# Log-sum-exp of 16384 rows: the order, cutting and summing of the last sixteen rows of each partition

## The chip, the cores and the metric

The kernel runs on one core of a Trainium2 chip. The metric is the device time of one execution in microseconds; for a kernel it is the median over its runs. A core has TensorE (matrix products, accumulating in PSUM), VectorE, ScalarE (activation functions), GpSimd and SyncE, each with its own instruction stream, and sixteen DMA engines that move data between HBM and the on-chip memory SBUF. Streams meet only at semaphores. SBUF has 128 partitions; "columns" below are fp32 elements of one partition, so that one column over all partitions is 512 bytes.

## The reference

```python
x = np.random.randn(32, 512, 1024).astype(np.float32)

def reference(x):
    max_x = np.max(x, axis=-1, keepdims=True)
    return (max_x.squeeze(-1) + np.log(np.sum(np.exp(x - max_x), axis=-1))).astype(np.float32)
```

The input is 67.1 MB, read once. The output has 16384 numbers.

## The kernel before

**Data and rows.** The 16384 rows of 1024 columns are spread over 128 partitions, 128 rows for each. The first 112 rows of a partition (`W`) are contiguous in HBM, and so are the last 16 (`B`), in a second region. The kernel exponentiates without subtracting a maximum, sums, and takes the logarithm. A check of all sums goes with it: TensorE adds a number to the PSUM cell `count` for each sum that is out of bounds, and adds the sums themselves, so that anything not finite shows; VectorE compares `count` with a bound, and only if it fails the whole work is done again, with the maximum, in a branch at the end. With the data here the branch isn't taken.

**The ring.** The rows land in `ring`, 48 rows of each partition. SyncE issues every load on one queue, in program order. Before a load it waits (`load`, L133 to 147) until whoever last used that stretch of the ring is done, as noted in `users`. Eighteen loads are listed in `LOADS`, with their size in rows and what is done with them; the first is cut in two. The first nine have 16, 16, 16, 16, 13.5, 12.5, 9, 7 and 6 rows, which makes 112. They lie at ring rows 0, 16, 32; 0, 16, 29.5; 0, 9, 16. The last 16 rows lie at ring rows 22 to 38, in nine loads of 4576, 3328, 2528, 1856, 1344, 992, 736, 544 and 480 columns.

**Sums.** ScalarE exponentiates in place (L235), one activation for a group or a load. Then, by letter:

- R: VectorE sums whole rows (L246).
- F: GpSimd adds the two halves of each row (L240), and VectorE sums the halves later (`reduce_folded`, L177).
- T: VectorE folds a row on itself in one instruction and gets its sum from the accumulator (L256). All but the last of the late 16 rows go this way.
- Y and Z: the last row is cut in 544 and 480 columns. ScalarE exponentiates each into PSUM and takes the sum from its own accumulator (L209), into `first_sum` and `last_sum`. VectorE copies the first to SBUF (L219).

A load may end within a row; the row is then summed after the load that completes it.

**The end.** After row 119 is queued ScalarE takes the log of the 112 early sums (L275), and VectorE checks 119 sums (L152, L157). SyncE stores the 112 results once the load ahead of the last has landed (L285). ScalarE then takes the log of 15 late sums (L288), and of the last row as Ln(last_sum + first_sum), the first part as the bias operand (L290). The store of the 16 (L294) waits for it. In parallel VectorE checks nine sums (L299), and takes the maximum of the last piece's input over a ceiling (L310), which stands for the check of `last_sum`; TensorE adds these (L305 to L315), VectorE compares (L317), ScalarE and VectorE read the flag and report to SyncE (`done`). SyncE clears the semaphores and waits last for the store (L378).

The order of each engine's work is written out by hand in one loop over the loads; `Counted.wait` leaves out a wait that the same engine has already made.

Of the kernel before, what the change touches and what calls it, by code (L numbers as in the profile page):

```python
# [12 lines left out]
LOW, HIGH = 1e-15, 1e15  # L13
CEILING = 27.0
STEEP = 2.0**48
RING = 48
B = 16
LATE = 119
# [3 lines left out]

LOADS = [
# [3 lines left out]
]  # L29
# [25 lines left out]
def kernel(  # L55
# [5 lines left out]
    nc = tc.nc  # L61
# [17 lines left out]
    LAST = NC - 1  # L79
# [14 lines left out]
    assert sum(size for size, _ in loads) == NC * d  # L94
    assert sum(s for _, ops in loads for _, s in ops) == NC
# [5 lines left out]
    sumexp = sbuf("sumexp", NC)  # L101
    res = sbuf("res", NC)
    clamped = sbuf("clamped", NC)
    bad = sbuf("bad", 3)
    over = sbuf("over", d)
    far = sbuf("far", 1)
    ones = sbuf("ones", 1)
    steep = sbuf("steep", 1)
    less = sbuf("less", 1)
    fine = sbuf("fine", 1, i32, 1)  # L110
    last_exp = nc.alloc_psum_tensor("last_exp", [P, d], fp32).ap()
    first_sum = nc.alloc_psum_tensor("first_sum", [P, 1], fp32).ap()
    last_sum = nc.alloc_psum_tensor("last_sum", [P, 1], fp32).ap()
    count = nc.alloc_psum_tensor("count", [1, 1], fp32).ap()

    landed = [nc.alloc_semaphore(f"landed{i}") for i in range(len(loads))]
# [13 lines left out]
    dve.did(nc.vector.memset(steep, STEEP))  # L130
    less_at = dve.did(nc.vector.memset(less, -CEILING * (loads[-1][0] // 2)))

# [16 lines left out]
    def check_early():  # L149
        dve.wait(act, summed_by_act)  # L150
        dve.wait(dve, dve.n)
        dve.did(nc.vector.tensor_scalar(  # L152
            out=clamped[:, 0:LATE], in0=sumexp[:, 0:LATE],
            scalar1=LOW, scalar2=HIGH, op0=ALU.max, op1=ALU.min,
        ))
        dve.wait(dve, dve.n)
        dve.did(nc.vector.scalar_tensor_tensor(  # L157
            out=clamped[:, 0:LATE], in0=clamped[:, 0:LATE], scalar=0.0, in1=sumexp[:, 0:LATE],
            op0=ALU.bypass, op1=ALU.not_equal, accum_out=bad[:, 0:1],
        ))  # L160
# [3 lines left out]
    def add_up(c, who, **kw):  # L164
        pe.wait(*who)
        return pe.did(nc.tensor.matmul(count, lhsT=ones, rhs=sumexp[:, c : c + 1], **kw))  # L166
# [16 lines left out]

    c = 0
# [4 lines left out]
    summed_by_act = 0  # L189
    ln_early = None  # L190
    first_loads = []
    for i, (size, ops) in enumerate(loads):
        if here + size > RING * d:
            assert here == p
            p = here = 0
        if any(q < here + size and q + t * d > here for _, t, q, _ in folded):
            reduce_folded()
        dma = load(i, here, done_before, size)
        if i < AHEAD:
            first_loads.extend(x.ins for x in dma)  # L200
        end = here + size
        done_before += size
        act.wait(landed[i], 16 * len(dma))
        for k, (how, s) in enumerate(ops):
            rows = ring[:, p : p + s * d].rearrange("p (c d) -> p c d", d=d)
            if how in "YZ":

                assert c == LAST and (how == "Z" or here == p)
                at = act.did(nc.scalar.activation(  # L209
                    out=last_exp[:, here - p : end - p], in_=ring[:, here:end], func=AF.Exp,  # L210
                    accum_out=first_sum if how == "Y" else last_sum,
                ))
                if how == "Z":
                    last_piece = ring[:, here:end]
                here = end
                if how == "Y":
                    nc.vector.addr_align(128, offset=0, max_nops=0)
                    dve.wait(act, at)
                    first_piece = dve.did(nc.vector.tensor_copy(out=sumexp[:, LAST:NC], in_=first_sum))  # L219
                summed_by_act = at  # L220
            elif how == "A":
                assert here == p
                v = ring[:, p : p + d]
                at = act.did(nc.scalar.activation(
                    out=v, in_=v, func=AF.Exp, accum_out=sumexp[:, c : c + 1]
                ))
                here += d
                users.append((p, p + d, act, at))
                summed_by_act = at
                who = (act, at)  # L230
            else:

                upto = end if k + 1 == len(ops) and c + s < LAST else p + s * d
                v = ring[:, here:upto]
                at = act.did(nc.scalar.activation(out=v, in_=v, func=AF.Exp))  # L235
                here = upto
            if how == "F":
                reduce_folded()
                pool.wait(act, at)
                at = pool.did(nc.gpsimd.tensor_tensor(  # L240
                    out=rows[:, :, 0:H], in0=rows[:, :, 0:H], in1=rows[:, :, H:d], op=ALU.add
                ))
                folded.append((c, s, p, at))
            elif how == "R":
                dve.wait(act, at)
                who = (dve, dve.did(nc.vector.reduce_sum(  # L246
                    out=sumexp[:, c : c + s], in_=rows, axis=AX.X
                )))
                users.append((p, p + s * d, *who))
            elif how == "T":  # L250
                if c >= W:
                    reduce_folded()
                dve.wait(act, at)
                for r in range(s):
                    lo = rows[:, r, 0:H]
                    who = (dve, dve.did(nc.vector.scalar_tensor_tensor(  # L256
                        out=lo, in0=lo, scalar=1.0, in1=rows[:, r, H:d],
                        op0=ALU.mult, op1=ALU.add, accum_out=sumexp[:, c + r : c + r + 1],
                    )))
                    users.append((p + r * d, p + (r + 1) * d, *who))  # L260
                    if c + r >= LATE:
                        add_up(c + r, who, start=False, stop=False)
            if how == "A" and c >= LATE:
                add_up(c, who, start=False, stop=False)
            if how in "RT":
                if c < W:
                    early_sum = dve.n
                reduce_folded()
            c += s
            p += s * d  # L270
            if c == LATE:

                act.wait(dve, early_sum)
                act.wait(act, early_act)
                ln_early = act.did(nc.scalar.activation(  # L275
                    out=res[:, 0:W], in_=sumexp[:, 0:W], func=AF.Ln
                ))
                check_early()
            if c <= W:
                early_act = summed_by_act  # L280
        assert here == end
# [6 lines left out]
    act.did(nc.scalar.activation(out=res[:, W:LAST], in_=sumexp[:, W:LAST], func=AF.Ln))  # L288
    act.wait(act, summed_by_act)
    ln_last = act.did(nc.scalar.activation(  # L290
        out=res[:, LAST:NC], in_=last_sum, func=AF.Ln, bias=sumexp[:, LAST:NC]
    ))
# [4 lines left out]

    dve.wait(dve, dve.n)
    dve.did(nc.vector.scalar_tensor_tensor(  # L299
        out=clamped[:, LATE:NC], in0=sumexp[:, LATE:NC], scalar=LOW,  # L300
        in1=sumexp[:, LATE:NC], op0=ALU.max, op1=ALU.not_equal, accum_out=bad[:, 1:2],
    ))
    add_up(LAST, (dve, first_piece), start=False, stop=False)
    pe.wait(dve, dve.n)
    pe.did(nc.tensor.matmul(count, lhsT=bad[:, 1:2], rhs=far, start=False, stop=False))  # L305
    pe.wait(dve, less_at)
    pe.did(nc.tensor.matmul(count, lhsT=less, rhs=steep, start=False, stop=False))
    half = last_piece.shape[1] // 2
    dve.wait(landed[-1], 16)
    dve.did(nc.vector.scalar_tensor_tensor(  # L310
        out=over[:, 0:half], in0=last_piece[:, 0:half], scalar=CEILING,
        in1=last_piece[:, half : 2 * half], op0=ALU.max, op1=ALU.max, accum_out=bad[:, 2:3],
    ))
    pe.wait(dve, dve.n)
    at = pe.did(nc.tensor.matmul(count, lhsT=bad[:, 2:3], rhs=steep, start=False, stop=True))  # L315
# [117 lines left out]
```

## Time and profile before

| | us |
|---|---|
| median of 3 runs | 161.59 |
| lowest, highest | 161.46, 161.63 |
| the profiled execution, its own time | 161.57 |
| its span in the profile | 160.2 |
| VectorE busy | 114.3 |
| ScalarE busy | 114.5 |
| GpSimd busy | 37.3 |
| TensorE busy | 2.2 |
| ScalarE idle, waiting for loads | 42.3 |

The span runs from the first to the last record of the core; the 1.4 us between span and time lie before and behind it. A row of a timeline gives the start, the duration, the engine, the line of the kernel, the operation, what is written and read, and the shapes. A row of the chain of waits gives start, duration and what the program's end waited for then. Rows marked SPq are DMA issues by SyncE; "KB, us" behind an issue of the page are its size and the time from issue to landing. Windows give, for each stretch, busy time of TensorE, its weight loads, VectorE, ScalarE and GpSimd, then the clock share, the DMA share and GB/s.

### The profile page before, as it was taken

The page shows a single profiled execution, that of the slowest core. Times are in us where ns is not written, and L with a number is a line of the kernel's source. Part 1 is how long each engine was busy: PE and PEld are TensorE (multiplying, and loading weights), DVE is VectorE, ACT ScalarE, POOL GpSimd, SP SyncE. Part 2 cuts the span into 40 slices and gives each one's busy share as a digit, 9 for nine tenths or more (in the row PEclk, how much of TensorE's full clock was granted, in tenths as well). Part 3 has the DMA queues.
Part 4 walks back from the last instruction along what each step waited for, and adds up shares of the span by engine and source line. Part 5 has one row for each costly group of instructions (what it writes and reads, how often), then busy time and mean ns, then how long its engine had stood idle before and what let it go on. Part 6 is the DMA issues. An engine that isn't in the chain of part 4 may idle for free.

```text
span 160.2 us, 221 instructions
## 1 busy us (share of the span) xinstructions
PE 2.2 (1%) x26; PEld 1.1 (1%) x26; DVE 114.3 (71%) x59; ACT 114.5 (71%) x31; POOL 37.3 (23%) x11
## 2 busy tenths in 40 slices
PE   0000000000000000000000000000000000000022
PEld 0000000000000000000000000000000000000011
DVE  0000000009999499994999859959999999999996
ACT  3000059980799708995099949992999989799996
POOL 0000000000000000000000994690004969891000
DMA  9996996996996996997999999999999999999992
GB/s 319 507 460 301 507 524 262 524 524 262 524 524 262 524 524 262 524 474 311 483 442 442 442 425 409 409 409 471 423 414 417 458 409 399 444 412 428 415 408 97
DMA packets 3025, 67.18 MB, mean 419 GB/s; under 512 B 592, under 2 KB 720, under 8 KB 1488
## 3 DMA queue, kind: packets, MB, share of 16 engines
q1 hardware_dynamic: 3024, 67.18, 97.8%
q14 instruction: 1, 0.01, 0.0%
HBM read 67.11 MB, written 0.07 MB: 419 GB/s over the span
## 4 chain that ended last, share of the span: by engine, by line
DMA 51%; ACT 28%; DVE 19%; issue 1%; PE 0%
DMA ring<-in_x_dram 51%; ACT ring L235 28%; DVE sumexp L246 16%; DVE sumexp L177 2%; DVE ring L256 1%; DVE over L310 0%; PE count L315 0%; ACT res L275 0%; DVE clamped L299 0%; DVE fine L317 0%; DVE sumexp L219 0%
## 5 line engine op out<-in xcount | busy, mean ns | idle before, releaser
L235 ACT ACTIVATE ring<-ring 128x16384 f32<-128x16384 f32 (+16 forms) x23 | 111.7, 4908 | 42.3 <-DMA ring<-in_x_dram 42.3
L246 DVE TENSOR_REDUCE sumexp<-ring 128x16 f32<-128x16384 f32 (+4 forms) x9 | 85.6, 9513 | 42.1 <-ACT ring L235 42.1
L240 POOL TENSOR_TENSOR ring<-ring 128x3072 f32<-128x3072 f32 (+3 forms) x7 | 37.1, 5315 | 107.2 <-ACT ring L235 107.2
L177 DVE TENSOR_REDUCE sumexp<-ring 128x6 f32<-128x3072 f32 (+3 forms) x7 | 18.4, 2659 | 0.0
L256 DVE SCALAR_TENSOR_TENSOR ring<-ring 128x512 f32<-128x512 f32 x15 | 9.6, 687 | 0.4 <-ACT ring L235 0.4
L127 ACT ACT_TABLE_LOAD x1 | 1.3, 1283 | 1.9 <-PEq L64 1.9
L162 PE MATMUL count<-far,bad 128*1 128x1 f32 x2 | 0.2, 164 | 153.0 <-DVE clamped L157 153.0
L166 PE MATMUL count<-sumexp,ones 128*1 128x1 f32 x18 | 1.6, 164 | 3.6 <-DVE ring L256 3.6
L128 DVE MEMSET ones<- 128x1 f32 x1 | 0.1, 59 | 2.0 <-PEq L64 2.0
L256 DVE DVE_READ_ACCUMULATOR ring<-ring 128x1 f32 x15 | 1.2, 82 | 0.0
L209 ACT ACTIVATE last_exp<-ring 128x544 f32<-128x544 f32 (+1 forms) x2 | 1.2, 588 | 0.0
L162 PEld LDWEIGHTS count<-far,bad 128*1 128x1 f32 x2 | 0.1, 82 | 153.0 <-DVE clamped L157 153.0
L166 PEld LDWEIGHTS count<-sumexp,ones 128*1 128x1 f32 x18 | 0.8, 81 | 4.4 <-DVE ring L256 4.4
L310 DVE SCALAR_TENSOR_TENSOR over<-ring 128x240 f32<-128x240 f32 x1 | 0.4, 404 | 0.0
L317 DVE TENSOR_SCALAR fine<-count 1x1 int32<-1x1 f32 x1 | 0.1, 147 | 0.3 <-PE count L315 0.3
L157 DVE SCALAR_TENSOR_TENSOR clamped<-clamped,sumexp 128x119 f32<-128x119 f32 x1 | 0.3, 283 | 0.0
L275 ACT ACTIVATE res<-sumexp 128x112 f32<-128x112 f32 x1 | 0.3, 279 | 0.0
L290 ACT ACTIVATE res<-last_sum,sumexp 128x1 f32<-128x1 f32 x1 | 0.3, 261 | 0.0
L209 ACT ACTIVATION_READ_ACCUMULATOR last_exp<-ring 128x1 f32 x2 | 0.3, 129 | 0.0
L152 DVE TENSOR_SCALAR clamped<-sumexp 128x119 f32<-128x119 f32 x1 | 0.2, 222 | 0.0
L288 ACT ACTIVATE res<-sumexp 128x15 f32<-128x15 f32 x1 | 0.2, 213 | 0.0
L299 DVE SCALAR_TENSOR_TENSOR clamped<-sumexp 128x9 f32<-128x9 f32 x1 | 0.2, 170 | 0.0
(17 smaller groups left out, 1.8 us busy)
## 6 DMA issues: line engine op xcount, KB each, us to landing
ring<-in_x_dram SPq DMA_DIRECT2D x1, 7936.0 KB, 21.3
ring<-in_x_dram SPq DMA_DIRECT2D x1, 6912.0 KB, 23.9
ring<-in_x_dram SPq DMA_DIRECT2D x1, 6400.0 KB, 19.7
ring<-in_x_dram SPq DMA_DIRECT2D x1, 4608.0 KB, 15.9
ring<-in_x_dram SPq DMA_DIRECT2D x1, 3584.0 KB, 24.0
ring<-in_x_dram SPq DMA_DIRECT2D x1, 3072.0 KB, 19.1
ring<-in_x_dram SPq DMA_DIRECT2D x1, 2288.0 KB, 24.2
ring<-in_x_dram SPq DMA_DIRECT2D x1, 1664.0 KB, 20.9
```

Of the source, the lines that this page charges most:

```text
L127: nc.scalar.preload_act_table_set("natural_log_exp_and_others")
L157: dve.did(nc.vector.scalar_tensor_tensor(out=clamped[:, 0:LATE], in0=clamped[:, 0:LATE], scalar=0.0, in1=sumexp[:, 0:LATE], op0=ALU.bypass ...
L162: pe.did(nc.tensor.matmul(count, lhsT=bad[:, 0:1], rhs=far, start=True, stop=False))
L166: return pe.did(nc.tensor.matmul(count, lhsT=ones, rhs=sumexp[:, c : c + 1], **kw))
L177: at = dve.did(nc.vector.reduce_sum(out=sumexp[:, c0 : c0 + s0], in_=halves, axis=AX.X))
L209: at = act.did(nc.scalar.activation(out=last_exp[:, here - p : end - p], in_=ring[:, here:end], func=AF.Exp, accum_out=first_sum if how == ...
L235: at = act.did(nc.scalar.activation(out=v, in_=v, func=AF.Exp))
L240: at = pool.did(nc.gpsimd.tensor_tensor(out=rows[:, :, 0:H], in0=rows[:, :, 0:H], in1=rows[:, :, H:d], op=ALU.add))
L246: who = (dve, dve.did(nc.vector.reduce_sum(out=sumexp[:, c : c + s], in_=rows, axis=AX.X)))
L256: who = (dve, dve.did(nc.vector.scalar_tensor_tensor(out=lo, in0=lo, scalar=1.0, in1=rows[:, r, H:d], op0=ALU.mult, op1=ALU.add, accum_out ...
L275: ln_early = act.did(nc.scalar.activation(out=res[:, 0:W], in_=sumexp[:, 0:W], func=AF.Ln))
L310: dve.did(nc.vector.scalar_tensor_tensor(out=over[:, 0:half], in0=last_piece[:, 0:half], scalar=CEILING, in1=last_piece[:, half : 2 * half ...
```

## The change

The last sixteen rows of a partition are loaded in another order and cut otherwise. With 0 to 16383 the columns of the sixteen rows, the nine late loads are, in this order: 11264 to 15792 (4528 columns), 480 to 3728 (3248), then 2512, 1824, 1328, 1072 and 800 columns from 3728 up to 11264, then 15792 to 16384 (592, the rest of row 15), and 0 to 480 (480, the start of row 0). They lie in the ring 32 columns further on, from ring row 22.03.

Row 15 and row 0 are thus cut in two, one part of each in an early load. VectorE sums those parts (432 and 544 columns) into `parts`. Behind the fifth late exponential ScalarE writes Ln(parts / 2) twice beside the place of row 15's last columns, and twice ahead of row 0's first columns. The last two exponentials run over their piece and these two elements, so that the exponential gives the two halves back and the piece's sum is the whole row's. Row 15's is summed by VectorE (a fold of 594 columns); row 0's by ScalarE's accumulator, over 482 columns, now into `sumexp` in SBUF.

One log of 16 sums stands at the end. The ceiling check, its two constants and the copy are gone. The early check covers the 112 sums and the two parts, the last check all 16 late sums. The loop's branches for T, Y, Z and A are gone; its first nine loads are as they were.

```diff
 LOADS = [
     (16, "R16"), (16, "R16"), (16, "R16"), (16, "F9 R7"), (13.5, "F6 R7"), (12.5, "R7 F6"),
-    (9, "R5 F4"), (7, "F4 R3"), (6, "F2 F2 R2"), (4.46875, "T4"), (3.25, "T3"), (2.46875, "T3"),
-    (1.8125, "T2"), (1.3125, "T1"), (0.96875, "T1"), (0.71875, "T1"), (0.53125, "Y"), (0.46875, "Z"),
+    (9, "R5 F4"), (7, "F4 R3"), (6, "F2 F2 R2"),
 ]
+HEAD, BACK, MID = 480, 592, 11
+PIECES = [2512, 1824, 1328, 1072, 800]
...
+    start = MID * d - sum(PIECES)
+    late = [(MID * d, B * d - BACK), (HEAD, start)]
+    for size in PIECES:
+        late.append((start, start + size))
+        start += size
+    late += [(B * d - BACK, B * d), (0, HEAD)]
...
+    def halves(v, c):
+        n = v.shape[1] // 2
+        return dve.did(nc.vector.scalar_tensor_tensor(
+            out=v[:, 0:n], in0=v[:, 0:n], scalar=1.0, in1=v[:, n : 2 * n],
+            op0=ALU.mult, op1=ALU.add, accum_out=c,
+        ))
...
+    base = p + GAP
+    joins = ring[:, base - 2 : base + B * d + 2]
+    summed = set()
+    seen = []
+    for k, (s, e) in enumerate(late):
+        i = len(loads) + k
+        [dma] = load(i, base + s, W * d + s, e - s)
+        act.wait(landed[i], 16)
+        v = ring[:, base + s : base + e]
+        if k == len(late) - 1:
+            act.wait(act, joined)
+            v = ring[:, base + s - 2 : base + e]
+            head_sum = act.did(nc.scalar.activation(
+                out=last_exp[:, 0 : e - s + 2], in_=v, func=AF.Exp, accum_out=sumexp[:, W : W + 1]
+            ))
+            break
+        if k == len(late) - 2:
+            act.wait(act, joined)
+            v = ring[:, base + s : base + e + 2]
+        at = act.did(nc.scalar.activation(out=v, in_=v, func=AF.Exp))
+        if k == 0:
+            reduce_folded()
+        dve.wait(act, at)
+        if k == len(late) - 2:
+            nc.vector.addr_align(128, offset=0, max_nops=0)
+            sums.append((NC - 1, dve, halves(v, sumexp[:, NC - 1 : NC])))
+            add_up()
+            continue
+        seen.append((s, e))
...
+        if k == 0:
+            halves(ring[:, base + (B - 1) * d : base + e], parts[:, 1:2])
+        if k == 1:
+            halves(ring[:, base + HEAD : base + d], parts[:, 0:1])
+            both = dve.n
+            act.wait(dve, early_sum)
+            ln_early = act.did(nc.scalar.activation(
+                out=res[:, 0:W], in_=sumexp[:, 0:W], func=AF.Ln
+            ))
+            check_early()
+        if k >= 1:
+            add_up()
+        if k == 4:
+            act.wait(dve, both)
...
+            joined = act.did(nc.scalar.activation(
+                out=to, in_=parts[:, :, None].to_broadcast([P, 2, 2]), func=AF.Ln, scale=0.5
+            ))
...
     act.wait(dve, dve.n)
-    act.did(nc.scalar.activation(out=res[:, W:LAST], in_=sumexp[:, W:LAST], func=AF.Ln))
-    act.wait(act, summed_by_act)
-    ln_last = act.did(nc.scalar.activation(
-        out=res[:, LAST:NC], in_=last_sum, func=AF.Ln, bias=sumexp[:, LAST:NC]
-    ))
+    act.wait(act, head_sum)
+    ln_last = act.did(nc.scalar.activation(out=res[:, W:NC], in_=sumexp[:, W:NC], func=AF.Ln))
     sp.wait(act, ln_last)
     nc.sync.dma_start(out=out_rest, in_=res[:, W:NC]).then_inc(stored, 16)
```

The part left out in the middle of the loop folds (`halves`) each of the rows 1 to 14 as soon as the loads seen so far cover it: four rows behind the first late load, then two, three, one, two, one and one.

More of the change, by code (lines that the diff above doesn't have):

```diff
@@ L93 @@
     ]
-    assert sum(size for size, _ in loads) == NC * d
-    assert sum(s for _, ops in loads for _, s in ops) == NC
+    assert sum(size for size, _ in loads) == W * d
+    assert sum(s for _, ops in loads for _, s in ops) == W
+    start = MID * d - sum(PIECES)
[4 more added lines that the diff above has]
+    late += [(B * d - BACK, B * d), (0, HEAD)]
+    assert start == MID * d and sum(e - s for s, e in late) == B * d
     def sbuf(name, cols, dtype=fp32, rows=P):
@@ L100 @@
     ring = sbuf("ring", RING * d)
-    sumexp = sbuf("sumexp", NC)
+    sums_all = sbuf("sumexp", 2 + NC)
+    parts, sumexp = sums_all[:, 0:2], sums_all[:, 2 : 2 + NC]
     res = sbuf("res", NC)
     clamped = sbuf("clamped", NC)
-    bad = sbuf("bad", 3)
-    over = sbuf("over", d)
+    bad = sbuf("bad", 2)
     far = sbuf("far", 1)
     ones = sbuf("ones", 1)
-    steep = sbuf("steep", 1)
-    less = sbuf("less", 1)
     fine = sbuf("fine", 1, i32, 1)
     last_exp = nc.alloc_psum_tensor("last_exp", [P, d], fp32).ap()
-    first_sum = nc.alloc_psum_tensor("first_sum", [P, 1], fp32).ap()
-    last_sum = nc.alloc_psum_tensor("last_sum", [P, 1], fp32).ap()
     count = nc.alloc_psum_tensor("count", [1, 1], fp32).ap()
-    landed = [nc.alloc_semaphore(f"landed{i}") for i in range(len(loads))]
+    landed = [nc.alloc_semaphore(f"landed{i}") for i in range(len(loads) + len(late))]
     act = Counted(nc, nc.scalar, "act")
@@ L157, in check_early @@
         dve.did(nc.vector.scalar_tensor_tensor(
[L158 removed]
+            out=clamped[:, 0:n], in0=clamped[:, 0:n], scalar=0.0, in1=sums_all[:, 0:n],
             op0=ALU.bypass, op1=ALU.not_equal, accum_out=bad[:, 0:1],
@@ L162, in check_early, with add_up @@
         pe.did(nc.tensor.matmul(count, lhsT=bad[:, 0:1], rhs=far, start=True, stop=False))
-    def add_up(c, who, **kw):
-        pe.wait(*who)
-        return pe.did(nc.tensor.matmul(count, lhsT=ones, rhs=sumexp[:, c : c + 1], **kw))
+    sums = []
+    def add_up():
+        while sums:
+            c, who, at = sums.pop(0)
+            pe.wait(who, at)
+            pe.did(nc.tensor.matmul(
+                count, lhsT=ones, rhs=sumexp[:, c : c + 1], start=False, stop=False
+            ))
     folded = []
@@ L205 @@
             rows = ring[:, p : p + s * d].rearrange("p (c d) -> p c d", d=d)
[L206 to L211, printed above, removed]
-                ))
[L213 to L236, printed above, removed]
+            upto = end if k + 1 == len(ops) else p + s * d
+            v = ring[:, here:upto]
+            at = act.did(nc.scalar.activation(out=v, in_=v, func=AF.Exp))
+            here = upto
             if how == "F":
@@ L243 @@
                 folded.append((c, s, p, at))
-            elif how == "R":
+            else:
                 dve.wait(act, at)
[L246 to L267, printed above, removed]
+                at = dve.did(nc.vector.reduce_sum(out=sumexp[:, c : c + s], in_=rows, axis=AX.X))
+                users.append((p, p + s * d, dve, at))
+                early_sum = at
                 reduce_folded()
@@ L270 @@
             p += s * d
[L271 to L280, printed above, removed]
-        assert here == end
+        assert here == end
+    assert c == W and here == p and p + GAP + B * d + 2 <= RING * d
@@ new lines @@
+    base = p + GAP
[17 more added lines that the diff above has]
+            v = ring[:, base + s : base + e + 2]
+        at = act.did(nc.scalar.activation(out=v, in_=v, func=AF.Exp))
+        if k == 0:
[7 more added lines that the diff above has]
+        seen.append((s, e))
+        for r in range(1, B - 1):
+            if r in summed:
+                continue
+            left = r * d
+            for s0, e0 in sorted(seen):
+                if s0 <= left < e0:
+                    left = e0
+            if left >= (r + 1) * d:
+                summed.add(r)
+                row = ring[:, base + r * d : base + (r + 1) * d]
+                sums.append((W + r, dve, halves(row, sumexp[:, W + r : W + r + 1])))
+        if k == 0:
[12 more added lines that the diff above has]
+            act.wait(dve, both)
+            to = bass.AP(
+                tensor=joins.tensor, offset=joins.offset, ap=[joins.ap[0], [B * d + 2, 2], [1, 2]]
+            )
+            joined = act.did(nc.scalar.activation(
+                out=to, in_=parts[:, :, None].to_broadcast([P, 2, 2]), func=AF.Ln, scale=0.5
+            ))
@@ L287 @@
     act.wait(dve, dve.n)
-    act.did(nc.scalar.activation(out=res[:, W:LAST], in_=sumexp[:, W:LAST], func=AF.Ln))
-    act.wait(act, summed_by_act)
-    ln_last = act.did(nc.scalar.activation(
-        out=res[:, LAST:NC], in_=last_sum, func=AF.Ln, bias=sumexp[:, LAST:NC]
-    ))
+    act.wait(act, head_sum)
+    ln_last = act.did(nc.scalar.activation(out=res[:, W:NC], in_=sumexp[:, W:NC], func=AF.Ln))
     sp.wait(act, ln_last)
     nc.sync.dma_start(out=out_rest, in_=res[:, W:NC]).then_inc(stored, 16)
+    sums.append((W, act, head_sum))
+    add_up()
     dve.wait(dve, dve.n)
+    dve.wait(act, head_sum)
     dve.did(nc.vector.scalar_tensor_tensor(
[L300 to L312, printed above, removed]
+        out=clamped[:, W:NC], in0=sumexp[:, W:NC], scalar=LOW,
+        in1=sumexp[:, W:NC], op0=ALU.max, op1=ALU.not_equal, accum_out=bad[:, 1:2],
     ))
     pe.wait(dve, dve.n)
-    at = pe.did(nc.tensor.matmul(count, lhsT=bad[:, 2:3], rhs=steep, start=False, stop=True))
+    at = pe.did(nc.tensor.matmul(count, lhsT=bad[:, 1:2], rhs=far, start=False, stop=True))
     dve.wait(pe, at)
```

14 lines of the change are left out of this document (4 added, 10 removed).

## The prediction

> **What bounds the kernel now.** I read the page first (busy line, chain of waits), then the timeline of ScalarE over the last 22 us, then SyncE's issues and the times to landing, then the DMA activity in fine slices.
>
> ```profile
> span 160.2 us, 221 instructions
> DMA  9996996996996996997999999999999999999992
> 138.06 12.36 ACT ring L235 x5
> 150.42 0.19 ACT res L275
> 150.61 6.04 ACT ring L235 x4
> ```
>
> The first two lines are the page's span and DMA share in 40 slices: the DMA engines are the limit over the run. The last three are the chain of waits: ScalarE takes a load at 138.06, and from there the chain is ScalarE without a gap. ScalarE's and SyncE's rows from there (start, duration):
>
> ```profile
> 143.51 4.02 ACT L235 ACTIVATE ring<-ring 128x4576 f32<-128x4576 f32 x1
> 147.44 2.98 ACT L235 ACTIVATE ring<-ring 128x3328 f32<-128x3328 f32 x1
> 150.33 0.28 ACT L275 ACTIVATE res<-sumexp 128x112 f32<-128x112 f32 x1
> 150.51 2.29 ACT L235 ACTIVATE ring<-ring 128x2528 f32<-128x2528 f32 x1
> 155.62 1.02 ACT L235 ACTIVATE ring<-ring 128x992 f32<-128x992 f32 x1
> 156.54 0.80 ACT L235 ACTIVATE ring<-ring 128x736 f32<-128x736 f32 x1
> 157.25 0.61 ACT L209 ACTIVATE last_exp<-ring 128x544 f32<-128x544 f32 x1
> 157.80 0.12 ACT L209 ACTIVATION_READ_ACCUMULATOR last_exp<-ring 128x1 f32 x1
> 157.85 0.57 ACT L209 ACTIVATE last_exp<-ring 128x480 f32<-128x480 f32 x1
> 158.34 0.13 ACT L209 ACTIVATION_READ_ACCUMULATOR last_exp<-ring 128x1 f32 x1
> 158.39 0.21 ACT L288 ACTIVATE res<-sumexp 128x15 f32<-128x15 f32 x1
> 158.51 0.26 ACT L290 ACTIVATE res<-last_sum,sumexp 128x1 f32<-128x1 f32 x1
> 158.79 0.34 SPq L294 DMA_DIRECT2D out_dram<-res  x1
> out_dram<-res SPq DMA_DIRECT2D x1, 8.0 KB, 1.4
> SPq L378 <- SPq L378: 0.3, 1, 0.3
> ```
>
> Each activation starts 0.06 to 0.10 us before the one ahead of it ends (736 columns end at 157.34, the next starts at 157.25): that is overlap, not waiting. The store goes out at 158.79 and lands 1.4 us later, 160.19, which is the span's end. SyncE's last wait (L378, 0.3 us, on the stored semaphore) says the same: the flag branch came in some 0.3 us earlier. So the end is: last exponential, accumulator read, two logs, store.
>
> ```profile
> 126.47 0.81 SPq L143 DMA_DIRECT2D ring<-in_x_dram  x2
> 135.53 0.80 SPq L143 DMA_DIRECT2D ring<-in_x_dram  x2
> 136.85 1.54 SPq L143 DMA_DIRECT2D ring<-in_x_dram  x1
> ring<-in_x_dram SPq DMA_DIRECT2D x1, 1664.0 KB, 20.9
> ring<-in_x_dram SPq DMA_DIRECT2D x1, 496.0 KB, 20.1
> ring<-in_x_dram SPq DMA_DIRECT2D x1, 240.0 KB, 20.9
> 155.00:156.00 1.00, 0.23 (x4) 0.09 (x2) 1.00 (x5) 1.00 (x2) 0.00 (x0) 1.00 1.01 403
> ```
>
> Issue plus time to landing: the 3328-column piece (1664 KB) lands at 126.47 + 20.9 = 147.37, the 992-column piece (496 KB) at 135.53 + 20.1 = 155.63, the last (240 KB) at 136.85 + 20.9 = 157.75. ScalarE takes them at 147.44, 155.62 and 157.85. So loads and ScalarE end level, with 0 to 0.1 us between them, and a change has to be costed on both.
>
> **The exponentials, resized.** Nine pieces before, nine after, 16384 columns in all, plus 4 for the joined elements. From 4576 columns (143.51 to 147.44, 3.93) and 736 (156.54 to 157.25, 0.71) a start-to-start step is 0.84 ns a column plus 0.09 us a piece. The sum over the pieces depends on columns and count alone: +4 columns, 0.003 us. As long as ScalarE never waits for a load, the new sizes cost nothing.
>
> **The joined log (added, on ScalarE between the 1328- and the 1072-column piece).** No such 2x2 write is in the trace. The nearest row is the 15-column log: 158.39 to 158.51, a step of 0.12. Bounds: 0 if it falls into a wait for a load, 0.28 (the whole early log) if nothing of it overlaps. I take 0.12, all on the path. Its own wait (VectorE's two partial sums) is over by 152.0, three microseconds earlier. Behind it on ScalarE stand only the last four exponentials.
>
> **One accumulator read less.** The next-to-last piece sums on VectorE now, so the read at 157.80 goes: its step is 157.85 - 157.80 = 0.05. The last exponential starts at 157.85 + 0.12 - 0.05 = 157.92, its read at 158.41.
>
> **One log at the end.** Before, the second log started 0.17 after the read (158.34 to 158.51), its release being the read's end; the 15-column log lay inside that gap. The new 16-column log needs the sum itself, so it starts at 158.41 + 0.17 = 158.58 and takes the 15-column log's 0.21 instead of 0.26: it ends at 158.79, the store is issued at 158.81 (0.02 behind, as before). The accumulator now goes to SBUF and not to PSUM, which no row shows; I give it 0, bounds -0.05 and +0.05 (the difference of the two log rows, one of which reads PSUM). The Trainium skill, ScalarE: Activation LUTs, What ACT_TABLE_LOAD costs, says that a [128,1] pointer operand adds some 93 ns to an ACTIVATE; the old last log has one as its bias. The rows show only 0.05 between the two logs; by the page's figure, estimated, the new end would be 0.04 earlier.
>
> **VectorE.** It takes over half of row 15 and of row 0, and the 594-column fold, for one 512-wide row fold, the copy and the ceiling check.
>
> ```profile
> 147.56 0.69 DVE L256 SCALAR_TENSOR_TENSOR ring<-ring 128x512 f32<-128x512 f32 x1
> 152.30 0.08 DVE L256 DVE_READ_ACCUMULATOR ring<-ring 128x1 f32 x1
> 152.88 0.69 DVE L256 SCALAR_TENSOR_TENSOR ring<-ring 128x512 f32<-128x512 f32 x1
> 158.28 0.40 DVE L310 SCALAR_TENSOR_TENSOR over<-ring 128x240 f32<-128x240 f32 x1
> 158.18 0.18 DVE clamped L299 x2
> 158.70 0.04 issue
> 158.74 0.19 PE L315 MATMUL count<-steep,bad 128*1 128x1 f32 x2
> 158.97 0.15 DVE fine L317
> ```
>
> The next fold starts where a read does, so a 512-wide fold steps 0.69 - 0.08 = 0.61, and (0.69 - 0.40)/272 is 1.05 ns a column, so 216 wide steps 0.31, 272 wide 0.36, 297 wide 0.39. Walking it through: four rows and the 216 from 147.56 end at 150.32; the second piece's exponential is done by then; two rows and the 272 end at 151.93, the early check (152.30 to 152.88 now, less the 0.08 read) at 152.5; three rows after the third exponential (152.7) and the fourth piece's one reach 155.2; two rows from 155.6, one, then one when the seventh exponential ends (157.45) reach 158.06. The eighth exponential (594 columns, 157.33 plus 0.68) ends at 158.01, so the 297-wide fold starts at 158.06 and its read ends at 158.53, where ScalarE's own read ends at 158.54. VectorE is therefore hidden by about 0.01 us only: without that cover, each delay of VectorE passes on in full. The flag: the check of 16 sums at 158.58, 0.18 with its read, 0.04 to TensorE, 0.23 to the compare as now (158.74 to 158.97): 159.03, so 0.06 late against 0.3 of cover.
>
> **The loads.** In the new order the first late load writes columns 11264 to 15792 of a region starting at ring row 22.03: ring rows 33.03 to 37.45. The old first late load took rows 22 to 26.47. Rows 36 to 42 hold the six GpSimd-folded rows of load 5, freed by a VectorE sum:
>
> ```profile
> 132.16 5.54 DVE L177 TENSOR_REDUCE sumexp<-ring 128x6 f32<-128x3072 f32 x2
> 118.95 0.33 SPq L143 DMA_DIRECT2D ring<-in_x_dram  x1
> 119.32 0.44 SPq L143 DMA_DIRECT2D ring<-in_x_dram  x1
> DMA  0099990099990099990059980999829992999829
> GB/s 0 0 0 0 0 0 0 0 0 0 143 164 123 20 41 246 246 369 369 389 2847 3318 1966 1905 0 635 0 0 0 0 0 0 0 0 0 0 0 0 0 0
> ```
>
> That sum is what the issue at 135.53 waited for. SyncE issues in order, so all nine late loads now wait for it: the first moves from 119.32 to 135.53, the others follow 0.45 us apart, done by 139.5. Meanwhile only load 8 is queued. The DMA line is 134 to 140 us in slices of 0.15: load 8's packets beat every 0.9 us, and the pattern changes at slice 20, 137.0, where load 9 took over. So the new load has 1.45 us from its issue to its first packet. The GB/s line is 0 to 4 us in slices of 0.1: the very first DMA, issued at 0.00, shows its first packets in slice 10, at 1.0 us, and full rate in slice 20, at 2.0 us. By the first packet the queue is refilled at 136.53, 0.45 before it runs dry; by full rate it is dry for 0.55. I take the first packet, since the start has a cold queue and 2 KB packets: cost 0, bounds 0 and 0.55. The Trainium skill, DMA: Bandwidth & Descriptors, speaks against this late issue: it gives a DMA about 2.0 us of fixed cost (Anatomy of one DMA, fitted there for the GpSimd path) and says to issue early so that it overlaps (Rules for kernel authors). It puts most of that behind the last byte, and a first byte from SyncE at 0.6 us (Specifications), by which nothing is lost.
>
> At 403 GB/s a column (512 B) takes 1.27 ns. Columns still to come behind each piece are 48, 128, 144, 176, 192, 112, 48, 0, 0 more than before, so the pieces land up to 0.24 us earlier and the last two when they did. ScalarE starts the last piece at 157.92 against its landing at 157.75: 0.17 of cover for the loads.
>
> **Sum.** Store path: +0.12 (joined log) - 0.05 (read) - 0.05 (shorter log) = +0.02 us. Span 160.22. The profiled execution took 161.57 for a span of 160.2, so 1.37 lies around it; 161.59, and as the median of the runs shown is 0.02 above that execution, 161.6.
>
> **The rivals.**
> *The queue runs dry* (slower side). Place: between load 8 and the first late load. For it: one DMA in flight for 16 us, and the ramp at the start of the run. Against: the first packets there at 1.0. It decides as soon as issue-to-flow exceeds 1.45 + 0.17 = 1.62 us; at the 2.0 of the ramp it costs 0.55 - 0.17 + 0.02 = +0.40, 162.0.
> *VectorE becomes the bound*. It has 0.01 us to spare; if its new narrow folds cost as much as a 512-wide row does (0.61 in place of 0.39 for the last), the log starts 0.2 later: 161.8. Against: the 240-wide row is visibly shorter.
> *The joined log is free, and the end is shorter*. If ScalarE is really paced by landings, the log falls into a wait: -0.05 - 0.05 = -0.10, or -0.15 with the accumulator's bound, 161.45. For it: landings and starts agree to 0.1 us. Against: steps of -0.06 to -0.10 everywhere, and pieces that now land earlier.
> *The change doesn't shorten the flag path to any effect*, though it drops the ceiling check: it has 0.3 of cover either way; if that cover isn't there, its +0.06 shows, 161.65, within the forecast's own range (161.45 to 161.8).
>
> **How the numbers follow.** The forecast (with the flag case) 0.53, the dry queue 0.23, VectorE 0.10, the free log 0.14. A measurement of this kernel can tell about 0.2%, 0.32 us, from no change. Of the dry queue 0.20 is slower by more and 0.03 within; of VectorE 0.04 slower; of the free log 0.07 faster by more, if more than the bounded terms goes; from the forecast 0.02 slower and 0.01 faster. Faster 0.08, same 0.66, slower 0.26. The range goes from 161.35 (free log, 0.1 below its sum) to 162.1 (dry queue, ramp bound and 0.1).
>
> **What would show it.** Right: first late issue at 135.5, the DMA share unbroken at 137, no ScalarE wait on a load after 138.06, a log of about 0.12 step ahead of the 1072-column piece, one 16-column log starting 0.17 after the last read, store issue at 158.8. Wrong: empty DMA slices around 137 and ScalarE waiting for the 4528-column piece; the 297-wide fold ending after the accumulator read; the last log held by VectorE; the flag's chain ending after the store's landing.

## The result, and the profile after

The changed kernel takes 164.06 us (median of 6 runs, 162.35 to 164.39) against 161.55 (6 runs, 161.46 to 161.74): a ratio of 1.013, with a 95% interval of 1.0083 to 1.0176. It is slower by about 2.5 us, outside the range of 161.35 to 162.1, and its runs spread over 2 us where those of before spread over 0.3. The profiled execution took 164.07, with a span of 162.7.

The first fence is the page after: the span, and the DMA share in 40 slices. The second is the chain of waits (start, duration, what the end waited for).

```profile
span 162.7 us, 244 instructions
DMA  8996999899699599599999999999999999999970
```

```profile
132.18 3.26 DVE sumexp L182
135.45 0.02 issue
135.46 0.02 SPq L51
135.48 0.05 issue
135.53 9.80 DMA ring<-in_x_dram
145.33 0.02 issue
145.35 6.83 ACT ring L257 x2
...
159.95 0.08 DVE ring L191
160.03 0.50 issue
160.53 0.09 DVE ring L191
160.63 0.30 issue
160.93 0.09 DVE ring L191
```

Two things are in it that the chain of before has not. VectorE's sum of the six folded rows ends, SyncE goes on, and one load takes 9.80 us from issue to landing, up to 145.33; before, the first late piece was taken at 143.51. And near the end there is half a microsecond of "issue", time in which VectorE waits for nothing that the profile shows. (The chain also books time inside a running fold as issue, 0.30 at 160.63 here and 0.55 at 157.44 in the chain before. During the half microsecond at 160.03 nothing runs on VectorE.) The waits of the changed kernel (who waited for whom: total, times, longest) name both:

```profile
SPq L51 <- DVE sumexp L182: 16.2, 1, 16.2
ACT ring L257 <- DMA ring<-in_x_dram: 1.8, 1, 1.8
ACT res L306 <- DVE ring L191: 0.6, 1, 0.6
DVE ring L191 <- issue: 0.5, 1, 0.5
```

The end of its timeline:

```profile
159.21 0.68 ACT L257 ACTIVATE ring<-ring 128x594 f32<-128x594 f32 x1
159.80 0.56 ACT L250 ACTIVATE last_exp<-ring 128x482 f32<-128x482 f32 x1
160.29 0.18 ACT L250 ACTIVATION_READ_ACCUMULATOR last_exp<-ring 128x1 f32 x1
160.53 0.47 DVE L191 SCALAR_TENSOR_TENSOR ring<-ring 128x297 f32<-128x297 f32 x1 [0.50 <-issue]
161.04 0.22 ACT L306 ACTIVATE res<-sumexp 128x16 f32<-128x16 f32 x1 [0.57 <-DVE ring L191]
161.28 0.34 SPq L308 DMA_DIRECT2D out_dram<-res  x1
```

The last exponential starts at 159.80 where 157.92 was forecast: 1.88 late. The log starts 0.75 behind the accumulator read instead of 0.17, since it waits for VectorE: 0.58 more. Together that is 2.46 of the 2.5 us.

The windows around the refill (busy time of TensorE, its loads, VectorE, ScalarE, GpSimd; clock, DMA share, GB/s), first of the kernel before, then of the changed one:

```profile
137.00:138.00 1.00, 0.00 (x0) 0.00 (x0) 1.00 (x2) 0.04 (x1) 1.00 (x1) 1.00 1.03 439
138.00:139.00 1.00, 0.00 (x0) 0.00 (x0) 1.00 (x1) 0.94 (x1) 1.00 (x1) 1.00 1.02 439
139.00:140.00 1.00, 0.00 (x0) 0.00 (x0) 1.00 (x1) 1.00 (x2) 0.34 (x1) 1.00 0.94 403
```

```profile
137.00:138.00 1.00, 0.00 (x0) 0.00 (x0) 1.00 (x2) 0.00 (x1) 1.00 (x1) 1.00 0.83 308
138.00:139.00 1.00, 0.00 (x0) 0.00 (x0) 1.00 (x1) 1.00 (x1) 1.00 (x1) 1.00 0.87 344
139.00:140.00 1.00, 0.00 (x0) 0.00 (x0) 1.00 (x1) 1.00 (x2) 0.28 (x2) 1.00 0.92 344
157.00:158.00 1.00, 0.19 (x2) 0.08 (x2) 0.71 (x3) 1.00 (x3) 0.00 (x0) 1.00 0.57 221
158.00:159.00 1.00, 0.38 (x4) 0.17 (x4) 1.00 (x5) 1.00 (x2) 0.00 (x0) 1.00 0.17 67
```

The DMA engines don't stop at 137; for three microseconds they run at 308 to 344 GB/s in place of 403 to 439, which is 285 KB less, some 0.7 us of the whole rate. Yet the first late piece is 1.8 late. The last two rows show why the two differ: some loads still run at 157 to 159, when the packets of the kernel before's last load had ended by 157.3.

The views give the DMA engines only as a sum. The packed trace behind them also holds the time of every packet and of the sixteen completion signals of each load, as many as there are engines. While the queue is full, sixteen packets are in flight at a time. In the kernel before it stays so when load 8 gives way to the first late load. In the changed one 11 are in flight at 137.5, 13 at 138.2, 15 at 138.9, and sixteen again from 139.05, 3.5 us after the issue. The signals of the first late load come between 143.00 and 143.49 before; in the changed kernel eleven come by 143.59, the other five at 144.01 to 145.33. Those of the last load are spread in the same way, 157.57 to 159.72 against 157.28 to 157.77 before. So a load has landed when the last of its sixteen shares is in, and the shares that start late here stay late to the end.

### The profile page after: what moved, and what is told of

It is laid out like the page before. It is cut to its first block, busy times and chain, and to the rows that moved or that the text cites. A ratio compares the mean times of both kernels' runs of the same rounds, so it can differ in the third digit from the quotient of the medians.

```text
span 162.7 us, 244 instructions
## 1 busy us (share of the span) xinstructions
PE 2.4 (1%) x36; PEld 1.3 (1%) x36; DVE 114.4 (70%) x58; ACT 114.6 (70%) x30; POOL 37.3 (23%) x11
## 4 chain that ended last, share of the span: by engine, by line
DMA 42%; ACT 34%; DVE 18%; another core or an unknown queue 3%; issue 1%; PE 0%; SPq 0%
DMA ring<-in_x_dram 42%; ACT ring L218 26%; DVE sumexp L229 14%; ACT ring L257 7%; DVE sumexp L182 2%; DVE ring L191 2%; PE count L169 0%; ACT res L284 0%; PE count L321 0%; DVE fine L323 0%; SPq L51 0%
## 5 line engine op out<-in xcount | busy, mean ns | idle before, releaser
L218 ACT ACTIVATE ring<-ring 128x16384 f32<-128x16384 f32 (+9 forms) x16 | 98.0, 6169 | 42.3 <-DMA ring<-in_x_dram 42.3
L257 ACT ACTIVATE ring<-ring 128x4528 f32<-128x4528 f32 (+7 forms) x8 | 14.4, 1853 | 1.8 <-DMA ring<-in_x_dram 1.8
L191 DVE SCALAR_TENSOR_TENSOR ring<-ring 128x512 f32<-128x512 f32 (+3 forms) x17 | 10.1, 642 | 2.8 <-ACT ring L257 2.3
L169 PE MATMUL count<-sumexp,ones 128*1 128x1 f32 x32 | 2.2, 164 | 4.5 <-DVE ring L191 4.5
L250 ACT ACTIVATE last_exp<-ring 128x482 f32<-128x482 f32 x1 | 0.6, 556 | 0.0
```

Source lines behind the costliest of these rows:

```text
L191: return dve.did(nc.vector.scalar_tensor_tensor(out=v[:, 0:n], in0=v[:, 0:n], scalar=1.0, in1=v[:, n : 2 * n], op0=ALU.mult, op1=ALU.add, ...
L250: head_sum = act.did(nc.scalar.activation(out=last_exp[:, 0 : e - s + 2], in_=v, func=AF.Exp, accum_out=sumexp[:, W : W + 1]))
```

## The experiments

Theory A: the first late load is issued too late, the queue runs dry, and the engines come back late. Theory B: the new cuts, their order or the shift by 32 columns make the loads slow. Theory C: VectorE's half microsecond comes from the alignment directive ahead of its last fold; theory D: from something else.

**e1_far_rows.** The late region moves to the end of the ring.

```diff
-GAP = 32
+GAP = 10208
```

> The late region moves to ring rows 31.97 to 47.97 (GAP 10208), so the first late load lies in rows that are free since 91 us and the second in rows free at 126.5; only the third waits until 135.5, with ten microseconds of loads still queued. Theory A (the queue runs dry because the first late load is issued at 135.5): the DMA activity around 137 to 140 us closes up, ScalarE takes the 4528-column piece at 143.5 with no wait, and the time falls to 161.6 to 162.1 (the upper end if the 0.5 us stall ahead of VectorE's last fold stays). Theory B (the new cuts and order, or the 128 bytes by which source and destination now differ, make the loads slow): cuts, order and a 128-byte difference are as in the changed kernel, so the time stays at 163.5 to 164.4.

162.17 us (7 runs, 162.01 to 162.48; ratio 1.0034, 1.0022 to 1.0045). ScalarE takes the first late piece with no wait, VectorE's stall is still there:

```profile
143.64 6.77 ACT L257 ACTIVATE ring<-ring 128x4528 f32<-128x4528 f32 x2
158.78 0.47 DVE L191 SCALAR_TENSOR_TENSOR ring<-ring 128x297 f32<-128x297 f32 x1 [0.50 <-issue]
```

One number gives back 1.9 us and the spread, and sixteen packets stay in flight through the change of load. Cuts, order and sums are those of the change; theory B falls.

**e2_before_late_issue.** The kernel before, with the issue made late and nothing else.

```diff
     def load(i, here, done_before, size):
+        if i == 9:
+            for a, b, who, at in users:
+                if a < 42 * d and b > 36 * d:
+                    sp.wait(who, at)
```

> The kernel before, whose first late load (4576 columns) waits in addition for the six folded rows of load 5, so that it is issued at 135.5 and not at 119.3. Cuts, order and sums are those of before. Theory A: the first late piece lands 1.5 to 2 us later than 143.5 and the time rises to 163.0 to 163.8, and spreads by more than a microsecond from run to run as the changed kernel's does. Theory B: the time stays within 0.3 us of 161.55.

163.22 us (162.88 to 163.95; ratio 1.0114, 1.0084 to 1.0143), with this row for the first late piece:

```profile
144.80 6.92 ACT L239 ACTIVATE ring<-ring 128x4576 f32<-128x4576 f32 x2 [1.25 <-DMA ring<-in_x_dram]
```

The wait alone makes the old kernel lose 1.6 us. In the profile, which is of the fastest run (162.88), the landing is 1.3 late, a little less than expected.

**e3_aligned_gap.** The alignment form of theory B.

```diff
-GAP = 32
+GAP = 128
```

> The changed kernel with GAP 128 in place of 32: source and destination of each late load are equal modulo 512 bytes again, and the first late load still waits until 135.5. Theory A: no change, 163 to 164.4 with the same spread. The alignment form of theory B: the loads speed up, 162 or below.

164.10 us (163.58 to 164.58; ratio 1.015, 1.012 to 1.018): no change. The 128 bytes play no part.

**e4_far_no_align.** e1 without the directive.

```diff
-            nc.vector.addr_align(128, offset=0, max_nops=0)
```

> e1_far_rows without the instruction that aligns VectorE's code ahead of the 297-wide fold. Theory C (the 0.5 us that VectorE stands still ahead of that fold, with its input ready, is code being loaded, and depends on where the instruction lies): the stall disappears, moves to another instruction or changes its length, and the time moves by up to 0.5 us against e1_far_rows. Theory D (the stall comes from the late loads or a semaphore): if e1_far_rows has it, so has this, with the same length.

162.65 us (162.53 to 162.78), slower than e1 by 0.5. The stall ahead of the fold is gone, the log starts at 158.60 where e1 had 159.29, and the time goes up all the same. The waits and issues of this kernel:

```profile
DVE clamped L315 <- issue: 0.3, 1, 0.3
SPq L383 <- SPq L383: 1.0, 1, 1.0
out_dram<-res SPq DMA_DIRECT2D x1, 8.0 KB, 2.5
```

A stall of 0.3 has moved to the accumulator read of the check behind the fold, and the last store takes 2.5 us to land where every other kernel here has 1.4. The stall ahead of the fold goes with the directive, as theory C says; what causes the new one of 0.3 stays open. The late store is another matter: of its sixteen completion signals fifteen are in by 160.26 and one comes at 161.31. An 8 KB packet of the queue that the page names "instruction" runs from 159.75 to 160.32, across the store's packets (159.69 to 160.37); in every other kernel it ends before they begin. That it held up the last signal fits, but no run tests it.

**e5_far_align_first.** The kernel before has the directive ahead of the wait (L217, L218), the changed one behind it.

```diff
+        if k == len(late) - 2:
+            nc.vector.addr_align(128, offset=0, max_nops=0)
         dve.wait(act, at)
         if k == len(late) - 2:
-            nc.vector.addr_align(128, offset=0, max_nops=0)
```

> e1_far_rows with two statements exchanged: the directive that aligns VectorE's code stands ahead of the wait for the eighth exponential, as it did in the kernel before, and not behind it. Theory C (at load time the directive becomes a branch over padding; behind the wait it runs only when the exponential is done, 0.64 us from that exponential's end to the fold's start): the fold starts within 0.1 us of the later of the exponential's end and VectorE's last read, the 16-column log starts about 0.5 earlier, the time is 161.6 to 161.8. Theory D (the stall belongs to the place in the code, whatever the order): the stall stays, 162.1 to 162.3.

161.67 us (11 runs, 161.61 to 161.79; ratio 1.0009, 1.0000 to 1.0018). Its timeline:

```profile
155.32 0.19 ACT L296 ACTIVATE ring<-sumexp 128x4 f32<-128x4 f32 x1
155.45 1.10 ACT L257 ACTIVATE ring<-ring 128x1072 f32<-128x1072 f32 x1
157.81 0.56 ACT L250 ACTIVATE last_exp<-ring 128x482 f32<-128x482 f32 x1
157.96 0.47 DVE L191 SCALAR_TENSOR_TENSOR ring<-ring 128x297 f32<-128x297 f32 x1
158.30 0.19 ACT L250 ACTIVATION_READ_ACCUMULATOR last_exp<-ring 128x1 f32 x1
158.58 0.22 ACT L307 ACTIVATE res<-sumexp 128x16 f32<-128x16 f32 x1
158.82 0.34 SPq L309 DMA_DIRECT2D out_dram<-res  x1
```

The fold follows the one before it with no gap. With issue and statement put right, what is left of the change is what it says it is, and it is worth nothing that a run can tell from no change.

**e6_align_first_alone.** The exchange alone, with GAP 32.

> The changed kernel (GAP 32, first late load issued at 135.5) with that exchange alone. Theory C, the two causes adding: 163.3 to 163.7, in the trace no 0.5 us stall of VectorE and a wait of ScalarE for the 4528-column piece of 1.3 to 2 us. If the stall hides behind the late loads: no change, 164.1.

163.78 us (162.86 to 164.26). Against 164.06 that is within the spread of both, so the time alone doesn't show it; the profile has no stall of VectorE and still a wait for the first late load:

```profile
144.61 6.82 ACT L257 ACTIVATE ring<-ring 128x4528 f32<-128x4528 f32 x2 [0.88 <-DMA ring<-in_x_dram]
```

The two causes are separate. That this profile's time, 162.86, is the lowest of its five runs goes with the short wait of 0.88.

**e7_before_lead_5us, e8_before_lead_2us.** The kernel before again, with the first late load held by a sum that ends at 132.2, and by a GpSimd operation that ends near 135.0.

```diff
+        if i == 9:
+            for a, b, who, at in users:
+                if a == 0:
+                    sp.wait(who, at)
```

```diff
+        if i == 9:
+            sp.wait(pool, 4)
```

> The kernel before, whose first late load waits in addition for VectorE's five-row sum of load 6, which ends at 132.2, some 4.8 us before load 8's packets end. Theory A: no loss, within 0.2 us of before. If it is the shallow queue as such, and not its running dry, that costs: 162.5 or more.

> The same with a wait for GpSimd's fourth operation, which ends at 134.84, 2.1 us before load 8's packets end, where e2_before_late_issue had 1.45 and lost 1.6. If the slowest DMA engine needs 1.45 + 1.25 = 2.7 us from issue to flow and the loss is what is missing of that: a loss of 0.5 to 1.1, 162.0 to 162.7. If the price is one restart, paid in full once the queue has run dry: either all of it (163.2) or nothing (161.6).

The issues, first of e7, then of e8:

```profile
132.29 0.33 SPq L147 DMA_DIRECT2D ring<-in_x_dram  x1
```

```profile
135.03 0.33 SPq L145 DMA_DIRECT2D ring<-in_x_dram  x1
144.68 6.96 ACT L237 ACTIVATE ring<-ring 128x4576 f32<-128x4576 f32 x2 [0.94 <-DMA ring<-in_x_dram]
```

With the kernel before and e2 this is a price list (the first of load 8's sixteen shares is through at 137.0, the last by 137.6 to 137.8):

| first late load issued at | ahead of 137.0 | median us | ratio, interval |
|---|---|---|---|
| 119.32 (before) | 17.7 | 161.5 to 161.6 | 1 |
| 132.29 (e7) | 4.7 | 161.55 | 1.0002 (0.9993 to 1.0011) |
| 135.03 (e8) | 2.0 | 162.76 | 1.0078 (1.0062 to 1.0093) |
| 135.50 (e2) | 1.5 | 163.22 | 1.0114 (1.0084 to 1.0143) |

A shallow queue costs nothing here (e7). Half a microsecond of earlier issue, from e2 to e8, buys 0.46 us by the medians, and 0.36 when each is compared with the kernel before as run beside it (161.64 and 161.54). Carried on at that slope, the loss would be gone at an issue some 3.2 to 3.6 us ahead. That is rough, since the two intervals overlap and no run lies between 2.0 and 4.7. The packets agree: in e7 sixteen stay in flight, in e8 all are back for good at 138.70, 3.7 us after the issue.

**e7b_before_wait_first.** The kernel before, with the statement order of the change.

```diff
-                    nc.vector.addr_align(128, offset=0, max_nops=0)
                     dve.wait(act, at)
+                    nc.vector.addr_align(128, offset=0, max_nops=0)
```

> The kernel before with the exchange the other way: VectorE's wait for the next-to-last exponential ahead of the alignment directive, as the changed kernel has it. Theory C (the directive's branch runs behind the wait): the copy that follows moves from 157.99 to 158.4 to 158.6; the flag path gets 0.5 later, against 0.3 of cover, and the last log may wait for the copy, so 161.7 to 162.0. If the stall belongs to the changed kernel's code alone: 161.5 to 161.6 and no gap.

162.13 us (161.93 to 162.32; ratio 1.004, 1.0025 to 1.0055):

```profile
158.55 0.16 DVE L219 COPY sumexp<-first_sum 128x1 f32<-128x1 f32 x1 [0.49 <-issue]
158.74 0.21 ACT L288 ACTIVATE res<-sumexp 128x15 f32<-128x15 f32 x1 [0.28 <-DVE sumexp L219]
```

The same stall appears in the old code when the wait stands first. It reaches ScalarE's first log, so the store goes out 0.34 later (159.13 for 158.79), and the flag 0.56 later. With e5 this shows theory C's main claim in both kernels: the half microsecond comes with a directive behind the wait and goes when it stands ahead of it. The packed trace also has what the views leave out, a branch in VectorE's stream. Here it runs from 158.00 to 158.05 and the copy starts 0.50 later; in the changed kernel from 159.98 to 160.03, and the fold starts 0.50 later. In the kernel before and in e5 it runs from 157.39 and 157.36, just after a fold of 0.69 has begun, so its half microsecond passes while VectorE is busy. e4, without the directive, has no branch there. So the directive is a branch at run time, and behind a wait the next instruction starts 0.50 us after its end. Why that long isn't shown: the one 8 KB "instruction" packet near the end begins 0.6 us after the stall is over (161.15 in the changed kernel, 159.17 here), so the stall is no wait for that packet.

**e8b_one_early_log.** e5 without the joined log; two partial sums ride with the early log, and GpSimd copies two elements. An unused place is filled with -200, whose exponential adds nothing.

```diff
-        if k == 4:
+        if k == 3:
...
+                out=logs[:, 0 : 2 + W], in_=sums_all[:, 0 : 2 + W], func=AF.Ln
...
+            pool.did(nc.gpsimd.tensor_copy(out=ring[:, base - 1 : base], in_=logs[:, 0:1]))
```

> e5_far_align_first without the joined log on ScalarE: the early log moves behind the fourth late exponential and takes the two partial sums with it (114 columns for 112), GpSimd copies the two logs to their places, one element each, and fills the odd place with -200, whose exponential adds nothing. The joined log's step of 0.13 on ScalarE goes: store issue 158.70 in place of 158.82, 161.5 to 161.6. If landings pace ScalarE there, or VectorE's last fold ends last, less comes of it: 161.6 to 161.7.

161.66 us (161.56 to 161.84; ratio 1.0009, 1.0000 to 1.0018), as e5. The last exponential starts at 157.79, 0.02 ahead of e5, though 0.13 of work is gone. The eighth exponential and SyncE's store that waits for that piece's landing start together:

```profile
157.20 0.68 ACT L257 ACTIVATE ring<-ring 128x594 f32<-128x594 f32 x1
157.20 0.35 SPq L303 DMA_DIRECT2D out_dram<-res  x1
```

So the loads pace ScalarE there. The completion signals say the same of e5: the load of the 1072-column piece is complete at 155.43, while the joined log runs (155.32 to 155.51), and that piece starts at 155.45. The joined log was free or nearly so.

**e9_before_late_issue_alone.** e2 with the second late load held until load 8 has landed.

```diff
+        if i == 10:
+            sp.wait(landed[8], 16)
```

> e2_before_late_issue with the second late load (and so all behind it) held until load 8 has landed at 138.0, so that the first late load's issue at 135.5 has no other issue behind it for 2.5 us. If the 1.6 us that e2_before_late_issue lost comes from the following issues working in the same queue while the engines wait for the first one's descriptors: the first late piece lands by 144.2 and the time falls to 162.3 or less. If each engine simply needs some 3 us from an issue to flow when its queue is dry: 163.2 again, first late piece at 144.7 or later.

163.07 us (10 runs): eight from 162.98 to 163.33, one at 164.05, one at 161.47. The time stays at that of e2, so the issues that follow are not the cause. (The profile is of the run at 164.05; there ScalarE takes the first late piece at 145.95.) The one run without any loss says that the price is not fixed: the same program, with the same late issue, can also come through whole.

## Why the prediction was wrong

**The refill: the place was found, the cost was not.** The prediction found that all nine late loads would now wait for the sum that ends at 135.5, and the issue stands at 135.53 as forecast. The step that failed is the cost of that late issue: "I take the first packet, since the start has a cold queue and 2 KB packets: cost 0, bounds 0 and 0.55". The rival *the queue runs dry* had the place and the sign, at 0.23, but a price of 0.40 where the runs have 1.6 (e2) to 1.9 (the change against e1). Both ends were aggregate rates of the sixteen engines: when the first packets flow, and when the sum reaches full rate. A landing is set by the last share, and neither row shows that one. The rows pointed to 2.0 us from issue to full rate at most; with load 8 still running it took 3.5 in the changed kernel and 3.7 in e8. The sign given for a dry queue, empty DMA slices around 137, didn't come: 11 of the sixteen shares ran on.

**VectorE: the cover was right, the delay was looked for in the wrong place.** "VectorE is therefore hidden by about 0.01 us only: without that cover, each delay of VectorE passes on in full" held: 0.50 of stall became 0.57 of wait for ScalarE. But the delay was put on narrow folds, which took what was forecast (e5: 297 columns, a step of 0.39 from 157.96 to the read at 158.35). The missed term is in the diff: the directive moved behind the wait. I read it as a line that moved with its code and gave it no cost; it costs the 0.50.

**What held.** Most of the store path, seen in e5, where both causes are gone: joined log, a step of 0.13 for 0.12 (155.32 to 155.45); store issue 158.82 for 158.81; flag compare at 159.06 for 159.03; time 161.67 for 161.6. That the sum came out is luck, though: two of its terms were off by 0.11 and cancelled. The joined log is not on the path, as the rival *the joined log is free* had it. In e5, and in the kernel before too, each late exponential starts 0.02 to 0.09 us behind the last completion signal of its load; the last one starts at 157.81 and not 157.92, and the 0.17 of cover for the loads is 0.05. And the accumulator read into SBUF takes 0.19 where the one into PSUM takes 0.13, with the log 0.28 behind its start and not 0.17; the bound of 0.05 given there was too small. (A slip without effect: 0.29/272 is 1.07 ns a column and not 1.05, and the 216-wide fold steps 0.30 for 0.31.)

**Issuing early.** The Trainium skill, DMA: Bandwidth & Descriptors, Rules for kernel authors, says to issue early and wait late; the price list agrees, from 0 to 1.6 us. The first-byte figure given there, 0.6 us (Specifications), was read as saying that nothing is lost; it speaks of a first byte, and the runs show that this is not what a late load costs.

## What to carry to other kernels

When a buffer's place in a ring changes, look up for each load which earlier reader it now waits for, and how far ahead of the queue's end it is issued: here 4.7 us were enough and 2.0 were not. Price a refill by the landing of a load, which its slowest share sets, and not by when the first bytes flow. And where code is aligned or jumped ahead of a critical instruction, let it stand ahead of the wait: that order cost nothing here, and the other half a microsecond.

## What the runs showed of the hardware

- A queue that is refilled 1.5 us before it ends costs 1.6 us and makes runs spread by a microsecond and more (162.35 to 164.39 in the changed kernel), with one run in ten of e9 that lost nothing. Some of the sixteen shares of the load come late (five in the changed kernel, by up to 1.7 us) and stay late in all the loads behind it. Which engines these are, and why they take this long, the trace doesn't show: its packets carry no engine.
- An alignment directive is a branch in VectorE's stream here. Behind a wait the next instruction starts 0.50 us after the branch, and VectorE stands still for that time (0.50 in the change, 0.49 in e7b); ahead of the wait the branch comes while a fold is running, and nothing is lost (e5, e6, the kernel before). In the change 0.64 us pass from the end of the exponential that the fold waited for (159.89) to the fold's start (160.53). Without the directive a stall of 0.3 turned up at the accumulator read of the check behind the fold (e4).
- SyncE can be held in an issue: 1.54 us at 136.85 before the change, and in it, at its fifth late load:

```profile
137.32 1.16 SPq L142 DMA_DIRECT2D ring<-in_x_dram  x1
```

Both end at 138.4 to 138.5, 0.4 to 0.5 us behind the landing of load 8 (138.04 and 137.97). In e1 no late issue took over 0.43 us, so what holds SyncE stays open, and no run prices it.
